# A matrix product with GELU on one core: groups 8 to 15 worked in pairs of the same block of A

## The chip, the cores and the metric

The kernel runs on 1 core of one Trainium2 chip. The metric is the device time of one execution in microseconds. Before the change it is 1500.78 us (median of 3 runs, 1499.52 to 1502.21).

## The reference

Two float32 matrices of 4096 x 4096 are multiplied and the tanh form of GELU is taken of the product.

```python
x = np.matmul(a, b)
return 0.5 * x * (1 + np.tanh(np.sqrt(2 / np.pi) * (x + 0.044715 * x**3)))
```

The kernel computes the product with float16 operands and float32 sums. It also sums the squares of the inputs, and a flag that it works out from them at the end decides whether a slower general path has to follow; in the runs here it does not.

## The kernel before

**Outer scheme.** A and B are each split into four quadrants (11, 12, 21, 22). Instead of eight products of quadrants the kernel makes seven, P1 to P7, after Strassen and Winograd: P1 and P2 are products of plain quadrants, the others take sums and differences of them. Of A these are S1 = 21 + 22, S2 = S1 - 11, S3 = 11 - 21 and S4 = 12 - S2; the products use P1: 11, P2: 12, P3: S4, P4: 22, P5: S1, P6: S2, P7: S3. The sums of B are worked out in the first groups and kept in DRAM as units (tiles `k_unit`, [128, 4, 2048] of float16, four cells of 512 KB each), so the later groups only fetch them.

**Groups.** A quadrant of A is 2048 rows high; it is worked in 4 blocks of 512 rows (mb), and a quadrant of B in 4 blocks of 512 columns (nb). A group is one pair (mb, nb): all seven products for 512 rows and 512 columns of each quadrant, 16 output tiles of 128 x 512. There are 16 groups in the order mb 0 to 3, four each; the blocks of B are taken in turned order, so that the last block of one mb is the first of the next. Group 0 is written out by hand (`first_group`), groups 1 to 6 load B and make its sums (`raw_group`), groups 7 to 15 fetch units (`late_group`).

**A product, uncut or cut.** One product is [512 x 2048] times [2048 x 512] into 4 PSUM banks, one for each row tile of 128. Uncut ("u") it is 4 quarters in K of 16 matmuls of 512 columns (`quarters`, `products`, L563): 64 matmuls. Cut, it is itself done by the seven-product scheme (`split`, `stage`, `part_pe`, L955): seven parts of 16 matmuls of 256 columns, 112 half-width matmuls in place of 64 whole ones. A cut product has 4 stages: stage 1 does part 1, stage 2 parts 2 and 5, stage 3 parts 6 and 7, stage 4 parts 3 and 4. Between them inner sums are made on VectorE (DVE), each 128 x 2048 float16 (`combine2`, L871):

- of A up to four: for part 5, then 6 and 3 (made in place of the one before), and 7 (`inner_sum`);
- of B four (`prepare` in `made_here`, mode "m", in place; `made_stored`, mode "ms", in other cells and stored to DRAM as pieces). Mode "f" fetches seven pieces instead, and "um" is an uncut product whose fetched unit is made into pieces beside it.

Where several groups of the same block of A cut the same product, the first can rewrite one quarter of the block in place (`BASE`, "make"), and the others ("made") need three inner sums of A instead of four. With a base, the sum for part 6 is not needed.

The parts are joined in PSUM: after part 1 its result (in the banks of region 21) is copied to region 11 and region 12 is set to zero (`copy_part`, L968, ScalarE, one instruction for each half bank, 128 x 256); after part 5 region 12 is copied out (j5); between parts 6 and 7 region 21 is copied out (j2); after part 7 two sums are added into the regions (`add_part`, L972, DVE, again one for each half bank). The first two matmuls of part 1 can be wide (`bits`): they run over 512 columns, which lets a following product add onto the whole bank.

**Order of the work.** PSUM has two sets of 4 banks, X and Y. Two products run interleaved (`run`, `both`): a stage or quarter of the one, then one of the other. In `late_group` these are two products of the same group: P1 with P2, P6 with P5, P7 with P3, and P4 alone or with the next group's P1 (`pending`). Their results are taken out by ScalarE (`copy_out`, L1166) or added on DVE (`add_bank`, L1172), then go through GELU (L1150) and a store on the queue of SP.

Everything from group 1 on is first listed with costs in `Plan` and then put in order by `schedule`: PE keeps the order in which products were listed; every other engine and both DMA queues (SP for stores, POOL for loads) take, at each step, the ready instruction with the earliest due time. The result is one fixed order of instructions for each engine. `MARGIN` is what the plan adds to the landing of a DMA before a DVE or ScalarE instruction counts as ready.

**Turning A.** Groups 7 and 11 load the next block of A in half blocks of 4 DMAs each through two free chunks (`turn_quad`); two DVE transposes (L440) and eight ScalarE weighings (L1206) of each half block follow.

**Cells.** SBUF holds 28 cells of 512 KB: 16 for B, 8 for S1 and S2, 4 for S3; there are 15 small tiles of 128 x 512 float32 (`y`).

Of the kernel before, what the change touches and what calls it, by code (L numbers as in the profile page):

```python
# [67 lines left out]
MARGIN = 0.6  # L68
# [21 lines left out]
def modes_of(tail=None, early=None, first4=None, **kw):  # L90
    got = {name: mode for mode, names in kw.items() for name in names.split()}
    return {**got, **{k: v for k, v in (("tail", tail), ("early", early), ("first4", first4)) if v}}


def bases_of(all_modes):
    got = {}
    for gs in (tuple(range(N_RAW, 8)), (8, 9, 10, 11), (12, 13, 14, 15)):
        early = [g for g in gs if all_modes[g].get("early") == "start"]
        turn = gs[-1] in TURNS
        for name in NAMES:  # L100
            if turn and (name in ("P2", "P6") or early and name in ("P1", "P5")):
                continue
            own = [g for g in gs if not (name == "P3" and (g in TURNS or g in early))]
            found = []
            while own and all_modes[own[-1]].get(name, "u") in ("f", "m", "ms"):
                found.append(own.pop())
            if len(found) > 1:
                for g in found:
                    got[g, name] = "made"
                got[found[-1], name] = "make"  # L110
    return got
# [16 lines left out]
TURNS = {7: 2, 11: 3}  # L128
# [191 lines left out]
def half_path(  # L320
# [39 lines left out]
    PS = [[psum_pool.tile([P, NC], F32, name="acc", tag=f"acc{k}{i}") for i in range(RT)] for k in range(2)]  # L360
# [65 lines left out]
    def turn_a(quad, c, h=None):  # L426

        x = slice(0, NX) if h is None else slice(h * NX // 2, (h + 1) * NX // 2)
        if (quad, c) == THIRD:
            n = NX // RT  # L430
            parts = [(slice(i * n, (i + 1) * n), staged[quad, c][i]) for i in range(x.start // n, x.stop // n)]
        else:
            parts = [(x, staged[quad, c][:, x, :])]
        for x, src in parts:
            transpose(a_slot[quad], c, x, src)

    def transpose(slot, c, x, src):
        dst = a_phys[slot, c].bitcast(U32).rearrange("p jj (mb q) -> p jj mb q", q=Q)
# [116 lines left out]
    def bank(s, i):  # L555
        return PS[s][i][:, :]
# [250 lines left out]

    def new_small():
# [22 lines left out]
    def fetch_unit(nb, name, q):  # L831
        x = new_cell()
        dma("POOL", cell(x), unit(nb, name)[:, q, :], [("u", nb, name, q)], [c(x)], "unit")
# [16 lines left out]


# [31 lines left out]
    def inner_sum(op, x, y, t=None):  # L883
        t = new_cell() if t is None else t
# [51 lines left out]
    def region(s, hw, r):  # L936
        h, w = int(hw[0]) - 1, int(hw[1]) - 1
        return PS[s][2 * h + r][:, w * HC : (w + 1) * HC], ("p", s, 2 * h + r)

    def part_pe(z, p):  # L940
# [8 lines left out]
        for r in range(2):  # L949
            i = 2 * h + r  # L950

            def fn(i=i, r=r):
                for j in range(NJ):
                    wide = p == "1" and j == 0 and z.bits
                    nc.tensor.matmul(  # L955
                        PS[s][i][:, :] if wide else PS[s][i][:, w * HC : (w + 1) * HC],
# [6 lines left out]
        if p in z.sum and p != "6" and z.last:  # L963
            free_cells.append(z.sum.pop(p))
# [4 lines left out]

    def add_part(dst, x, y):  # L970
        (d, dt), (xa, xt), (ya, yt) = dst, x, y
        dve("part", lambda: nc.vector.tensor_tensor(out=d, in0=xa, in1=ya, op=ALU.add), [xt, yt], [dt])  # L972

    def stage(z, k):
        s = z.s

        def of(hw, r):
            return region(s, hw, r)

# [4 lines left out]
        if k == 1:  # L984
# [7 lines left out]
            for r in range(2):  # L992
                copy_part(of("11", r), of("21", r))
            for r in range(2):
                copy_part(of("12", r), (zeros[:, 0:1].to_broadcast([P, HC]), None), "zero")
            z.prepare(1)
        elif k == 2:
            part_pe(z, "2")
            x5 = z.sum["5"]
            part_pe(z, "5")  # L1000
            if z.last:
                free_cells.remove(x5)
# [182 lines left out]
    def turn_quad(mb, quad, slot, pairs):  # L1185
# [3 lines left out]
        for h in range(2):  # L1189
# [9 lines left out]
            for cc in range(CH):  # L1199
                src = s.rearrange("p x (c r) -> p c x r", c=CH)[:, cc]  # L1200
                x = slice(h * n, (h + 1) * n)
                dve("turn", lambda cc=cc, x=x, src=src: transpose(slot, cc, x, src), toks, [("a", slot, cc, h)])
            f = new_small()
            for x in range(n):
# [3 lines left out]
                    toks, [("rows", ih), ("f", f)], batch=("w", mb, quad, h), slack=60.0)  # L1208
# [135 lines left out]
    def raw_group(gi, keep_units, makes, fetch=(), next_nb=None, turn=None, pending=None):  # L1344
# [47 lines left out]
        if turn:  # L1392
# [4 lines left out]
            turn_quad(turn, "11", slots["a"]["21"], (24, 26))  # L1397
# [23 lines left out]
        if turn:  # L1421
            turn_quad(turn, "12", slots["a"]["11"], (24, 26))
# [16 lines left out]
        if turn:  # L1439
            turn_quad(turn, "21", slots["a"]["12"], (24, 26))  # L1440
# [37 lines left out]
        def p4_ends():  # L1478
            if turn:
                turn_quad(turn, "22", slots["a"]["22"], (24, 26))  # L1480
# [46 lines left out]
    sets, held_sums = {"X": 0}, []  # L1527
    BASE = bases_of(GROUPS)

    def late_group(gi, modes, turn=None, pending=None):  # L1530

        mb, nb = groups[gi]
        new_mb = gi == N_RAW or groups[gi - 1][0] != mb
        last = gi == LAST
        X, Y = sets["X"], 1 - sets["X"]
        cut = {name for name in NAMES if modes.get(name, "u") in ("f", "m", "ms")}
        p4_first = bool(turn) or "first4" in modes
        if p4_first:
            cut.discard("P4")
        tail_v = "P7" in cut or "P3" in cut and modes.get("tail") == "v" or "P4" in cut  # L1540
        tail_v = tail_v or pending is not None and not p4_first
        if gi == N_RAW:
            for q in range(QPH):
                copy_quarter(ST[q], raw("21"), q)
        elif new_mb:
            block(SA, 1, raw("21"), raw("22"))
        if new_mb or not held_sums:
            block(SB, -1, blk(SA), raw("11"))
        s3 = ST
        if new_mb and gi != N_RAW:  # L1550
            block(ST, -1, raw("11"), raw("21"))
        def early():
            k = new_unit()
            turn_quad(groups[gi][0] + 1, "11", slots["a"]["21"], (k[0], k[2]))
            free_cells.extend(k)

        held_sums.clear()
        s4_in_slot = not turn and modes.get("early") != "start"
        if modes.get("early") == "start":
            early()  # L1560
        if s4_in_slot:
            if new_mb:
                s4 = raw("21")
                for q in range(QPH):
                    dst, toks = a_quarter(s4, q)
                    combine2(dst, toks, a_quarter(raw("12"), q), a_quarter(blk(SB), q), -1)
            held_sums.append(gi)
        if turn:
            k = new_unit()
            pairs = (k[0], k[2])  # L1570

        def fourth():
            if not s4_in_slot:
# [318 lines left out]
```

## Time and profile before

| | before |
|---|---|
| median of the runs shown | 1500.78 us |
| the profiled execution | 1500.4 us |
| its span | 1498.5 us |
| mean granted TensorE clock | 0.998 |
| PE, DVE, ACT, POOL busy | 1483.8, 1207.5, 708.8, 452.6 us |
| matmuls | 9886 |
| DMA traffic | 388.76 MB |

The span runs from the first to the last instruction; the profiled execution's own time is 1.9 us longer. PE is the row of the matmuls, PEld the weight loads that run beside them. Matmuls are pipelined, so the mean length of one (379 ns for 512 columns) is not the time between two; that is read from the chain of work or from a stretch of the timeline, by the start of the first and the number that follow. In the rows of groups, the number behind the bar is the idle time of that engine just before those instructions, with what ended it.

### The profile page before, as it was taken

The numbers are of one execution on the slowest core, as the hardware profiler recorded it, in microseconds if no ns is written. First come the engines' busy times: TensorE is split into PE (matmuls) and PEld (weight loads), VectorE is DVE, ScalarE is ACT, GpSimd is POOL, SyncE is SP. The second block draws the span as 40 slices with busy tenths as digits, with TensorE's granted clock in tenths as the row PEclk, the third lists the DMA queues.
The fourth block names the chain that finished last, engine by engine and source line by source line (L and its number), as shares of the span: only waits on it lengthen the run. The fifth ranks groups of instructions, "written<-read, shape, count | busy, mean of one in ns | idle before, by whom it ended". The sixth has DMA issues, their size and how long they took to land.

```text
span 1498.5 us, 26219 instructions
## 1 busy us (share of the span) xinstructions
PE 1483.8 (99%) x9886; PEld 967.4 (65%) x9886; DVE 1207.5 (81%) x1476; ACT 708.8 (47%) x1606; POOL 452.6 (30%) x822
## 2 busy tenths in 40 slices
PE   9999999999999999999999999999999999999997
PEld 4444554444445446555665888887765778888886
DVE  2598778246499889686799999998699889998887
ACT  5445246363954645546663242436654234242433
POOL 7766342451204415212330212122331112112220
PEclk9999999999999999999999999999999999999999
DMA  9999799999979999997997777889997747698974
GB/s 177 193 204 224 135 247 314 292 279 268 249 269 250 284 356 254 309 264 239 252 330 297 269 265 241 299 272 215 305 283 288 259 141 264 209 336 279 327 257 182
DMA packets 200918, 388.76 MB, mean 259 GB/s; under 512 B 20304, under 2 KB 110416, under 8 KB 200784
## 3 DMA queue, kind: packets, MB, share of 16 engines
q0 software_dynamic: 139296, 231.79, 65.3%
q1 hardware_dynamic: 61488, 155.22, 27.5%
q8 instruction: 79, 1.29, 0.3%
q14 instruction: 55, 0.45, 0.1%
HBM read 315.62 MB, written 155.19 MB: 314 GB/s over the span
## 4 chain that ended last, share of the span: by engine, by line
PE 90%; DMA 5%; POOL 2%; DVE 1%; ACT 1%; issue 1%; DVEq 0%; ACTq 0%; POOLq 0%
PE acc L563 47%; PE acc L955 43%; DMA stage<-in_a_dram 2%; DMA bR<-k_unit 2%; POOL bR L465 1%; POOL stage L465 1%; DVE bR L871 0%; POOL aD L465 0%; DVE y L1172 0%; DMA out_dram<-y 0%; ACT stage L474 0%; DMA aD<-in_a_dram 0%; DMA bR<-in_b_dram 0%; ACT y L1150 0%; ACT y L1206 0%
## 5 line engine op out<-in xcount | busy, mean ns | idle before, releaser
L563 PE MATMUL acc<-bR,aT 128*128 128x512 f16 x1792 | 393.6, 379 | 1.0 <-DVE y L1172 0.6
L871 DVE TENSOR_TENSOR bR<-bR 128x2048 f16<-128x2048 f16 (+1 forms) x292 | 344.7, 1203 | 47.1 <-PE acc L955 23.6
L789 POOL DMA_DIRECT2D bR<-k_unit x258 | 143.7, 559 | 629.7 <-PE acc L955 359.3
L563 PE MATMUL acc<-bR,aD 128*128 128x512 f16 x1472 | 322.4, 379 | 0.0
L563 PEld LDWEIGHTS <-aT 128*128 128x128 f16 x1856 | 181.6, 98 | 215.0 <-issue 1.6
L955 PE MATMUL acc<-bR 128*128 128x256 f16 x2640 | 307.3, 273 | 1.5 <-ACT y L968 1.5
L955 PEld LDWEIGHTS <-bR 128*128 128x128 f16 x2640 | 258.3, 98 | 33.6 <-issue 1.6
L563 PEld LDWEIGHTS <-aD 128*128 128x128 f16 x1568 | 153.3, 98 | 182.5 <-DVE aD L548 1.2
L1172 DVE TENSOR_TENSOR y<-acc,y 128x512 f32<-128x512 f32 x324 | 209.0, 684 | 36.0 <-ACT y L1166 14.7
L789 POOL DMA_DIRECT2D bR<-in_b_dram x288 | 155.5, 545 | 252.5 <-DMA bR<-in_b_dram 102.2
L955 PE MATMUL acc<-bR,aT 128*128 128x256 f16 (+1 forms) x1696 | 201.0, 274 | 0.0
L968 ACT COPY y<-acc 128x256 f32<-128x256 f32 x220 | 81.6, 372 | 238.2 <-PE acc L955 235.4
L955 PEld LDWEIGHTS <-aT 128*128 128x128 f16 x1696 | 166.0, 98 | 24.4
L1150 ACT ACTIVATE y<-y 128x512 f32<-128x512 f32 x200 | 119.9, 626 | 109.0 <-DVE y L1172 108.7
L1240 ACT ACTIVATE y<-bR 128x1024 bf16<-128x1024 f16 x128 | 129.8, 1052 | 66.0 <-DVE y L1245 51.9
L1245 DVE TENSOR_TENSOR y<-y 128x1024 bf16<-128x1024 bf16 x120 | 82.1, 686 | 41.6 <-ACT y L1240 40.1
L955 PE MATMUL acc<-bR,aD 128*128 128x256 f16 (+1 forms) x944 | 110.9, 273 | 0.0
L955 PE MATMUL acc<-bR,stage 128*128 128x256 f16 (+1 forms) x880 | 105.7, 274 | 0.0
L955 PEld LDWEIGHTS <-aD 128*128 128x128 f16 x944 | 92.4, 98 | 12.1
L955 PEld LDWEIGHTS <-stage 128*128 128x128 f16 x880 | 86.1, 98 | 15.1
L871 DVE TENSOR_TENSOR bR<-aT 128x2048 f16<-128x2048 f16 x66 | 80.3, 1217 | 18.2 <-PE acc L563 18.2
L1166 ACT COPY y<-acc 128x512 f32<-128x512 f32 x80 | 45.9, 586 | 103.2 <-PE acc L563 65.4
(89 smaller groups left out, 1223.4 us busy)
## 6 DMA issues: line engine op xcount, KB each, us to landing
bR<-k_unit POOLq DMA_DIRECT2D x258, 512.0 KB, 7.0
out_dram<-y SPq DMA_DIRECT2D x252, 256.0 KB, 7.0
k_unit<-bR SPq DMA_DIRECT2D x112, 512.0 KB, 8.8
bR<-in_b_dram POOLq DMA_DIRECT2D x384, 128.0 KB, 6.9
k_piece<-bR SPq DMA_DIRECT2D x40, 512.0 KB, 4.7
bR<-in_a_dram POOLq DMA_DIRECT2D x64, 256.0 KB, 8.9
stage<-in_a_dram POOLq DMA_DIRECT2D x48, 256.0 KB, 7.7
bR<-k_piece POOLq DMA_DIRECT2D x24, 512.0 KB, 7.7
```

Of the source, the lines that this page charges most:

```text
L465: nc.gpsimd.dma_start(out=dst, in_=src)
L563: nc.tensor.matmul(acc, sa[:, j // 2, i * P : (i + 1) * P, j % 2], sb[:, j, :], start=start and j == 0, stop=stop and j == 3, skip_group_c ...
L789: return plan.add(queue, COST[queue], lambda: eng.dma_start(out=dst, in_=src), r=r, w=w, size=MOVE[what] * SPREAD, weight=weight, **kw)
L871: nc.vector.tensor_tensor(out=dst, in0=xa, in1=ya, op=ALU.add if op > 0 else ALU.subtract)
L955: nc.tensor.matmul(PS[s][i][:, :] if wide else PS[s][i][:, w * HC : (w + 1) * HC], sa[:, j // 2, r * P : (r + 1) * P, j % 2], rhs(j, wide) ...
L968: act(cost, lambda: nc.scalar.copy(out=d, in_=x), [xt] if xt else [], [dt])
L1150: act("gelu", lambda: nc.scalar.activation(t, t, ACT.Gelu_apprx_tanh), [("f", f)], [("f", f)])
L1166: act("copy", lambda: nc.scalar.copy(out=sm(f), in_=bank(s, i)), [], [("f", f), ("p", s, i)])
L1172: dve("add", lambda: nc.vector.tensor_tensor(out=sm(g), in0=bank(s, i), in1=sm(f), op=ALU.add), [("f", f)], [("f", g), ("p", s, i)])
L1240: act("square", lambda t=t, src=src: nc.scalar.activation(t, src, ACT.Square), [c(cx)], [("f", f)], slack=60.0)
L1245: dve("add16", lambda t=t, u=u: nc.vector.tensor_tensor(out=u, in0=u, in1=t, op=ALU.add), [("f", f)], [("f", e)], slack=60.0)
```

## The change

Groups 8 to 15 are worked in pairs of groups that have the same block of A: 8 and 9, 10 and 11, 12 and 13, 14 and 15. `late_pair` runs each product for both groups, one on each set of banks, interleaved: P1, P2, P6, P5, P3, P7, P4. Group 7 keeps the old way (`lone_group`).

- Where both groups cut a product, the second uses the inner sums of A that the first had made (`lead`); the sum that is made in place waits until both are through the part before. In stage 2 the second group does part 5 before part 2.
- Where both leave a product uncut, the two run one behind the other.
- An uncut product adds onto what is in its banks; where the product before was cut, the running sum is first copied back into the bank (`seed`).
- The PSUM sets become one tile of four banks each, and four of the joins are done for two banks in one instruction: the copy to region 11, the zero, the copy j5, and each of the two adds. The copy j2 stays in halves.
- The running sum u of both groups (8 small tiles) is stored to DRAM after P5 (`park`) and loaded back after P3 (`unpark`). Two cells of B become four more small tiles.
- The block of A is turned during groups 7 and 10/11; in the pair through one chunk only. S1, S2, S3 and S4 of a new block are made by 16 sums at its start (`fill`); in the turning pair S4 is made over S2 after P6.
- `MARGIN` goes from 0.6 to 0.2.
- The tables say anew which products are cut and how, in the raw groups too, and which pieces groups 4 and 5 make; `bases_of` looks at whole pairs of pairs.

```diff
-MARGIN = 0.6
+MARGIN = 0.2
 def bases_of(all_modes):
...
+    for a, b in ((8, 10), (12, 14)):
         for name in NAMES:
+            if b == 10 and name in ("P2", "P3", "P6"):
                 continue
...
+            if all(all_modes[g].get(name, "u") in ("f", "m", "ms") for g in (a, a + 1, b, b + 1)):
+                got[a, name], got[b, name] = "make", "made"
-RAW_MAKES = {4: ("P1", "P4", "P3"), 5: ("P2",)}
-RAW_CUT = {4: "P7", 5: "P7 P3", 6: "P7", 2: "", 1: "P7"}
+RAW_MAKES = {4: ("P6", "P5", "P2"), 5: ("P4",)}
+RAW_CUT = {4: "P3", 5: "P7", 6: "P7", 2: "", 1: "P3"}
 GROUPS = {
-    7: modes_of(m="P1 P6", ms="P7", tail="v"),
-    8: modes_of(f="P7", m="P3 P4 P6", ms="P5", um="P2"),
-    9: modes_of(f="P3", m="P1 P4 P5 P6 P7", ms="P2"),
-    10: modes_of(m="P1 P2 P3 P5 P7", ms="P6", early="end"),
-    11: modes_of(m="P1 P2 P6 P7", tail="v"),
-    12: modes_of(m="P4 P6 P7", ms="P5", tail="v"),
-    13: modes_of(f="P7", m="P1 P2 P3 P4 P5 P6"),
-    14: modes_of(f="P3", m="P2 P6 P7", ms="P1 P4 P5"),
-    15: modes_of(f="P2 P6", m="P1 P4 P5 P7", ms="P3", tail="v", first4=True),
+    7: modes_of(m="P1 P6", um="P4", tail="v"),
+    8: modes_of(m="P2 P3 P4 P5 P6 P7", ms="P1"),
+    9: modes_of(f="P5", m="P2", ms="P6 P7", um="P3"),
+    10: modes_of(f="P4", m="P1 P2 P5 P6 P7"),
+    11: modes_of(m="P1 P4 P5 P7"),
+    12: modes_of(m="P1 P2 P3 P4 P6", ms="P5 P7"),
+    13: modes_of(f="P1", m="P2 P3 P4 P5 P7", ms="P6"),
+    14: modes_of(f="P2 P3 P6", m="P4 P5 P7", ms="P1"),
+    15: modes_of(m="P1 P2 P3 P5 P6", ms="P7"),
 }
-TURNS = {7: 2, 11: 3}
+EXTRA = (14, 15)
+PARK = (8, 10, 12, 14)
+TURNS = {7: 2, 10: 3}
...
-    PS = [[psum_pool.tile([P, NC], F32, name="acc", tag=f"acc{k}{i}") for i in range(RT)] for k in range(2)]
+    PS = [psum_pool.tile([P, RT, NC], F32, name="acc", tag=f"acc{k}") for k in range(2)]
...
             part_pe(z, "1")
-            for r in range(2):
-                copy_part(of("11", r), of("21", r))
-            for r in range(2):
-                copy_part(of("12", r), (zeros[:, 0:1].to_broadcast([P, HC]), None), "zero")
+            copy_pair(pair_of("11"), pair_of("21"))
+            copy_pair(pair_of("12"), (zeros[:, 0:1].unsqueeze(2).to_broadcast([P, 2, HC]), []))
...
-            part_pe(z, "2")
             x5 = z.sum["5"]
-            part_pe(z, "5")
+            for p in "25" if z.first else "52":
+                part_pe(z, p)
...
-            for r in range(2):
-                copy_part(j(z.j5, r), of("12", r))
+            copy_pair(pair_j(z.j5), pair_of("12"))
...
-            for r in range(2):
-                add_part(of("12", r), of("12", r), j(j2, r))
+            add_pair(pair_of("12"), pair_of("12"), pair_j(j2))
...
-            for r in range(2):
-                add_part(of("22", r), of("21", r), j(z.j5, r))
+            add_pair(pair_of("22"), pair_of("21"), pair_j(z.j5))
...
+    def late_pair(ga, turn):
+        gs = (ga, ga + 1)
...
+        if groups[ga - 1][0] != mb:
+            fill("S1", 1, "21", "22")
+            fill("S2", -1, "S1", "11")
+            fill("S3", -1, "11", "21")
+            if not turn:
+                fill("21", -1, "12", "S2")
...
+        def both(name, fresh, dones, bits):
+            lists, cuts, lead = [], [], None
+            for s in range(2):
...
+                shared = is_cut(0, name) and is_cut(1, name)
+                z = split(s, source[name], b, bits(s), BASE.get((ga, name)) if shared else None, lead)
+                lead = z if shared else None
+                lists.append(stages_of(z, lambda i, s=s: dones(s, i)))
...
+        new_a("11", "21")
+        both("P1", lambda s: True, p1_done, uncut("P2"))
+        new_a("21", "11")
+        if last:
+            final_answer()
+        both("P2", cut("P2"), p2_done, uncut("P6"))
+        both("P6", cut("P6"), p6_done, uncut("P5"))
+        if last:
+            final_read()
+        if turn:
+            fill("S2", -1, "12", "S2")
+        new_a("22", "12")
+        both("P5", cut("P5"), p5_done, uncut("P3"))
+        if ga in PARK:
+            park()
+        new_a("12", "S1")
+        both("P3", cut("P3"), p3_done, lambda s: False)
+        if ga in PARK:
+            unpark()
+        both("P7", lambda s: True, p7_done, uncut("P4"))
+        both("P4", cut("P4"), p4_done, lambda s: False)
```

More of the change, by code (lines that the diff above doesn't have):

```diff
@@ L1525, in raw_group @@
         return later_
-    sets, held_sums = {"X": 0}, []
     BASE = bases_of(GROUPS)
[L1530 to L1535, printed above, removed]
-        cut = {name for name in NAMES if modes.get(name, "u") in ("f", "m", "ms")}
[L1537 to L1573, printed above, removed]
-                block(SB, -1, raw("12"), blk(SB))
@@ L1726, in late_group, with c22, c21 @@
[L1726 removed]
+            f = new_small()
+            add_bank(v[i], X, i, f)
+            out_of(gi, i, 1, 1, f)
+        def c22(i):
+            f = copy_out(X, i)
+            add_bank(f, Y, i)
+            out_of(gi, i, 1, 1, f)
+        def c21(i):
+            add_bank(x4[i], X, i)
+            out_of(gi, i, 1, 0, x4[i])
+        run(work("P4", Y, True, p4_done))
+        turn_quad(turn, "22", raw("22"), pairs)
+        turn_quad(turn, "11", blk(ST), pairs)
```

379 lines of the change are left out of this document (199 added, 180 removed).

## The prediction

> **What bounds the kernel now.** The first view to read is the page's table of busy times, because its shares say which engine can set the end at all, and then the waits of PE, which say whether that engine ever stood still.
>
> ```profile
> PE 1483.8 (99%) x9886; PEld 967.4 (65%) x9886; DVE 1207.5 (81%) x1476; ACT 708.8 (47%) x1606; POOL 452.6 (30%) x822
> DVE  2598778246499889686799999998699889998887
> DMA  9999799999979999997997777889997747698974
> ...
> PE acc L955 <- ACT y L968: 1.5, 1, 1.5
> PE acc L572 <- DVE table L744: 1.5, 1, 1.5
> PE acc L598 <- ACT y L581: 0.7, 1, 0.7
> PE acc L563 <- DVE aD L548: 0.7, 1, 0.7
> PE acc L563 <- DVE y L1172: 0.6, 1, 0.6
> PE acc L598 <- DMA bR<-in_b_dram: 0.4, 1, 0.4
> PE acc L563 <- DMA bR<-k_unit: 0.4, 1, 0.4
> PE acc L563 <- ACT y L581: 0.4, 1, 0.4
> ```
>
> PE waits 6.2 us in the whole span. L572 and L598, and the waits on aD at L548 and y at L581, belong to the first group, which the change leaves alone; what is left after it is 1.5 + 0.6 + 0.4 = 2.5 us. A busy PE could still be a slow one, so the next view is the chain that ended last, where runs of matmuls show their pace without a gap, and the groups by form, which count the matmuls.
>
> ```profile
> 178.27 1.96 PE acc L955 x16
> 707.43 1.75 PE acc L955 x16
> 1130.77 3.45 PE acc L563 x16
> 1134.23 3.49 PE acc L955 x32
> ...
> L955 PE MATMUL acc<-bR,aT 128*128 128x512 f16 x24 | 9.1, 379 | 0.0
> L955 PE MATMUL acc<-bR,stage 128*128 128x512 f16 x14 | 5.3, 379 | 0.0
> L955 PE MATMUL acc<-bR,aD 128*128 128x512 f16 x2 | 0.8, 379 | 0.0
> L968 ACT COPY acc<-zero 128x256 f32<-128x256 f32 x110 | 41.1, 375 | 3.1
> ```
>
> One quarter of an uncut product (16 matmuls of 512) takes 3.45 us, so an uncut product takes 4 x 3.45 = 13.80 us. Two parts of a cut product (32 matmuls of 256) take 3.49 us, so its seven parts take 3.5 x 3.49 = 12.22 us, and a cut is worth 1.58 us of PE. Where the first matmuls of part 1 are wide, the part takes 1.96 instead of 1.75 us: 0.21 us more. Two zero copies stand in each cut product, so 110 of them are 55 cuts, and two wide matmuls stand in each wide one, so 24 + 14 + 2 = 40 are 20 wide cuts. This checks against GROUPS and RAW_CUT: 5 cuts in the raw groups, 50 in groups 7 to 15.
>
> Since PE is paced by its own matmuls nearly everywhere, a change can win only three things: matmul time, the 2.5 us of late waits, and what follows the last matmul. The tail is in the timeline of the last stretch.
>
> ```profile
> 1484.30 7.33 DVE L1172 TENSOR_TENSOR y<-acc,y 128x512 f32<-128x512 f32 x12
> 1485.01 7.28 ACT L1150 ACTIVATE y<-y 128x512 f32<-128x512 f32 x12 [3.35 <-DVE y L1172]
> 1488.08 1.91 PE L955 MATMUL acc<-bR,aT 128*128 128x256 f16 x16
> ```
>
> The last matmul ends at 1488.08 + 1.91 = 1489.99, the last add at 1491.63, the last gelu at 1492.29, and the span at 1498.5 with the last store.
>
> **The change, part by part.**
>
> Matmuls. Counting the names in the new tables: raw groups 4 cuts (was 5), group 7 two (was 3), groups 8 to 15 7 + 4 + 6 + 4 + 7 + 7 + 7 + 6 = 48 (was 47). That is 54 against 55, +1.6 us. A cut product starts wide where the next product in its banks adds onto it: the 4 raw ones, P6 of group 7, and in the pairs P1 of 11, P5 of 9, 10 and 11, P7 of 9 and 15, so 11 against 20: 9 x 0.21 = -1.9 us. Together -0.3 us on the path. The order of the products is free on PE.
>
> Tail. Now 12 adds in 7.33 us, 0.61 each, are queued on DVE around the last parts, and the last one ends 1.64 us behind the last matmul. In the new order the last thing is the fourth quarter of group 15's uncut P4, whose four row tiles end 0.86 us apart (3.45/4), each with one add; only one add is left behind the last matmul, 0.68 us by the row of L1172 below. I take -0.9 us; the bounds are 0 and -1.6.
>
> DVE. The groups by form give busy time, mean ns of one, and idle time before; the last two rows are one of the windows (busy PE, PEld, DVE, ACT, POOL, then clock, DMA share, GB/s) and one of the chain.
>
> ```profile
> L871 DVE TENSOR_TENSOR bR<-bR 128x2048 f16<-128x2048 f16 x284 | 339.8, 1218 | 47.1 <-PE acc L955 23.6 <-PE acc L563 9.2 <-DMA bR<-in_b_dram 6.4
> L1172 DVE TENSOR_TENSOR y<-acc,y 128x512 f32<-128x512 f32 x324 | 209.0, 684 | 36.0 <-ACT y L1166 14.7 <-PE acc L955 10.8 <-PE acc L563 5.6
> L972 DVE TENSOR_TENSOR acc<-acc,y 128x256 f32<-128x256 f32 x220 | 83.8, 424 | 10.2 <-ACT y L968 5.2 <-PE acc L955 4.4
> L968 ACT COPY y<-acc 128x256 f32<-128x256 f32 x220 | 81.6, 372 | 238.2 <-PE acc L955 235.4
> L1166 ACT COPY y<-acc 128x512 f32<-128x512 f32 x80 | 45.9, 586 | 103.2 <-PE acc L563 65.4 <-issue 20.1 <-PE acc L955 17.1
> ...
> 800.00:1000.00 200.00, 200.00 (x1767) 172.59 (x1765) 194.70 (x243) 73.39 (x175) 37.19 (x67) 1.00 0.75 264
> 1473.70 4.62 DVE bR L871 x4
> ```
>
> Of A, a cut product makes four inner sums (three where a base is "made"). Before: 50 late cuts, 25 of them "made", and one more shares (P4 of 14 and 15): about 200 - 25 - 3 = 172 sums. After: 21 products are shared by both groups of a pair, 8 of these "made", and 8 cuts stand alone: 13 x 4 + 8 x 3 + 8 x 4 = 108. So 64 sums go, at 4.62/4 = 1.16 us each 74 us of DVE. The sums of B stay (44 cuts make theirs, 6 fetch them, as before). The joins: four adds of 424 ns become two of the 128x512 form, 684 ns, 1.70 to 1.37 us per cut; on ACT six copies of about 372 become three of about 586 with j2 still in halves. All of this is worth nothing on the path: in the row 800:1000 DVE is busy 194.7 of 200 us while PE is busy 200.00, so PE does not wait even for a full DVE. If that cover went, it would be where DVE is fullest in the new kernel, the pair 12 and 13: 52 sums of B, 28 of A, 16 for the blocks of A, 28 joins and 56 adds, 96 x 1.16 + 84 x 0.61 = 162 us against 14 x 12.22 = 171 us of PE, 95%, under the 97% that the row shows covered.
>
> A pair operation reads or writes two banks, so it cannot start until both row tiles of the part are done. Timed from the start of two interleaved cuts: part 1 of the first ends at 1.75, the two-bank copy and the zero follow (two of 586 ns, at 2.9), and part 2 wants the banks at 3.5, after part 1 of the second. 0.6 us is left; I count 0, and above 0 only where ACT is late (below). The page "PSUM — Partial Sum Buffer" of the Trainium skill (PSUM bank collisions raise a hardware error) has it that engines are to be kept apart by whole bank and not by address, so that PE stays out of both banks until the copy and the zero are done, though part 2 writes only a half of each. By that rule the 0.6 us is all there is; by address the zero would not matter and 1.2 us would be left, and the sum is the same by both. No row here shows PE and ACT in one bank at once.
>
> Shared sums. This adds a wait that the old kernel did not have. Without a base (P2 and P6 of 8/9, P1 and P4 of 10/11, P4 of 12/13) the sum for part 6 is made in place of the sum for part 5, once the second group is through part 5. By the times above: second group's stage 2 begins at 7.0, its part 5 (now first) ends at 8.75, the sum of 1.22 us ends at about 10.0, and the first group's part 6 starts at 10.5. Before, the same sum had from 7.0 on. The sum for part 3 behind part 6 has the same half microsecond. Behind it on DVE wait the sums of B for part 7. It costs 0 if DVE is free at that moment, and if it is in the middle of another sum up to 1.16 - 0.5 = 0.66 us, at 10 places: 0 to 6.6 us, and no gain. I take 0, by the nearest row (a DVE at 97% with no PE wait).
>
> Moves. Parking u adds 4 x 8 stores on SP and as many loads on POOL, of 256 KB. The page's DMA lines and a window beside them:
>
> ```profile
> DMA packets 200918, 388.76 MB, mean 259 GB/s; under 512 B 20304, under 2 KB 110416, under 8 KB 200784
> ...
> out_dram<-y SPq DMA_DIRECT2D x252, 256.0 KB, 7.0
> ...
> 700.00:800.00 100.00, 100.00 (x630) 61.49 (x629) 81.86 (x94) 63.59 (x165) 31.19 (x57) 1.00 1.01 292
> ```
>
> That is 16.8 MB more over some 690 us, 24 GB/s. A parked tile is back after two landings of 7.0 us, and P3's two products (24 us) lie between; the queue of POOL issues 8 more in a stretch where it is 30% busy. In 700:800 the DMA engines are busy without a break and PE still does not wait. Cost 0, bounds 0 and one wait of 0.4 us per pair (as the wait on k_unit above), 1.6 us. The page "DMA: Bandwidth & Descriptors" (Specifications) speaks against this part: it gives HBM about 358 GB/s per core. By it the 24 GB/s on top of a slice at 292 still fits and the sum stays; the fastest slice, 356 GB/s in the page of before, would not have room.
>
> Waits behind a DMA. MARGIN goes from 0.6 to 0.2 us, so DVE and ACT instructions that read fresh data are queued closer to its landing, and A is turned through one chunk instead of two. What that costs when it fails is in the waits: the 1.5 us at L968.
>
> ```profile
> 1125.57 0.63 ACT L1206 ACTIVATE y<-bR 128x512 f16<-128x512 f16 x1 [2.97 <-DMA bR<-k_unit]
> 1128.46 0.63 ACT L968 COPY y<-acc 128x256 f32<-128x256 f32 x2
> 1128.87 1.91 PE L955 MATMUL acc<-bR 128*128 128x256 f16 x16 [1.48 <-ACT y L968]
> ```
>
> A weighing of A stood 2.97 us on ACT, the copy out of the bank queued behind it came late, and PE stood 1.48 us. The new kernel has the same 16 half blocks of A to turn behind group 6. I take the three late waits (2.5 us) as replaced by as much, net 0; the bounds are -2.5 and +9 (six such waits more).
>
> **Sum.** -0.3 - 0.9 + 0 = -1.2 us. The profiled execution took 1500.4 us (span 1498.5), so 1499.2 there; its median of runs is 1500.78, 0.4 above, so 1499.6.
>
> **Rivals.** A: all late waits go, the freed DVE being early everywhere. Then -1.2 - 2.5 = -3.7, 1497.1 us. For it: 74 us less on DVE. Against: two of the three waits (1.5 and 0.4) hang on a DMA, and DVE's relief does not move a landing. Lower than this it cannot go by much, as the matmuls stay.
>
> B, on the other side: the shared sums without a base are late. One place is nothing; from 7 of the 10 places (4.6 us) on, it outweighs the 1.2 us and 3 us more. At all ten 1499.6 + 6.6 = 1506.2 us. For it: 0.5 us of room, where a sum takes 1.16. Against: the row 800:1000, where DVE is 97% full and no sum came late for PE.
>
> C, also slower: landings are late by more than the new margin and ACT's weighings hold the copies, 1.5 us each as in the row above. From three more on it is slower; six give 1499.6 + 9 = 1508.6 us. For it: 0.4 us less margin, one chunk, 16.8 MB more. Against: before, with a full queue, it happened once.
>
> **Numbers.** My forecast, no change in effect, 0.45. A 0.2. B 0.14, C 0.16; 0.05 for something in neither. A measurement of this kernel tells about 0.2%, 3 us. Faster 0.21, same 0.45, slower 0.34. The likeliest case alone goes from 1497.8 to 1503.8. The range reaches over A and to the end of C: 1496.6 to 1508.6.
>
> **What would show it.** The matmuls: 110 zero copies of 128x256 become 54 of 128x512, and the wide matmuls at the line of the parts are 22. The tail: one add after the last matmul. DVE near 1207 - 83 = 1125 us busy. PE's waits: few, none above 1.5 us; B shows as waits of PE's part 6 or 3 on a DVE sum in pairs 8, 10 and 12, C as waits on an ACT copy behind a weighing in group 7 or pair 10, or on k_unit. The forecast is wrong if PE's late waits sum to more than 7 us or to less than 1.

## The result and the profile after

The kernel after takes 1846.13 us (median of 4 runs, 1845.62 to 1848.18), the kernel before beside it 1500.15 us (4 runs, 1498.86 to 1502.21). The ratio is 1.2307, with an interval from 1.2286 to 1.2329: 23% slower. The profiled execution took 1845.62 us with a span of 1844.1 us, so 345.6 us more span than before.

The page of the kernel after, with the busy times, and the busy tenths of PE over 40 slices of the span:

```profile
PE 1550.4 (84%) x9838; PEld 963.5 (52%) x9838; DVE 1115.3 (60%) x1260; ACT 691.3 (37%) x1452; POOL 470.7 (26%) x854
...
PE   8778888888888898888888888888988878787876
```

PE, 99% busy before, is 84% busy, and DVE and ACT have lower shares than before too: no engine has become the bound. The loss is spread over the whole span: already the second slice shows 7, and it belongs to the first group. So the pairs cannot be the cause alone. A stretch of 640 us that lies ahead of the first pair in the kernel after, and ahead of group 8 in the kernel before, in the windows of both kernels (columns: busy us and count of PE, PEld, DVE, ACT, POOL, then clock, DMA share, GB/s); of the kernel after:

```profile
60.00:700.00 640.00, 550.31 (x2602) 254.33 (x2601) 374.68 (x414) 267.01 (x525) 199.52 (x366) 1.00 0.88 210
```

and of the kernel before:

```profile
60.00:700.00 640.00, 638.28 (x3229) 315.67 (x3227) 480.70 (x560) 331.11 (x629) 230.57 (x423) 1.00 1.05 261
```

The clock is 1.00 in both, and 2602 matmuls are done instead of 3229. What PE stood for is in its waits (us in total, times, longest), kernel after:

```profile
PE acc L964 <- DVE y L1187: 58.3, 61, 1.4
PE acc L964 <- ACT y L978: 34.0, 73, 0.7
PE acc L964 <- DVE acc L997: 32.4, 28, 1.2
PE acc L559 <- ACT y L1181: 29.9, 43, 1.2
PE acc L559 <- ACT y L1175: 23.6, 33, 1.2
PE acc L559 <- DVE y L1187: 21.8, 25, 1.4
...
PE acc L594 <- DVE y L573: 10.6, 13, 0.8
```

All lines of this view together are 375 waits and 287.0 us, against 8 waits and 6.2 us before. Nearly all of the releasers are instructions that read or write PSUM: the adds onto results, the copies out, the joins. Hardly any of them was late before, and L594 with L573 is the first group, whose code the change leaves as it was, but for the PSUM line and the way its banks are addressed.

What such a wait looks like is in the timeline of the first group (start, duration, engine, line, instruction, and in brackets the idle time before it and its releaser). Kernel after:

```profile
18.74 0.59 ACT L577 COPY y<-acc 128x512 f32<-128x512 f32 x1
...
19.38 1.02 PE L594 MATMUL acc<-bR,aT 128*128 128x512 f16 x4 [0.67 <-ACT y L577]
...
20.43 0.59 ACT L577 COPY y<-acc 128x512 f32<-128x512 f32 x1 [1.11 <-PE acc L594]
21.07 1.02 PE L594 MATMUL acc<-bR,aT 128*128 128x512 f16 x4 [0.68 <-ACT y L577]
```

and the same place before:

```profile
15.63 10.74 PE L598 MATMUL acc<-bR,aT 128*128 128x512 f16 x49
...
18.54 1.76 ACT L581 COPY y<-acc 128x512 f32<-128x512 f32 x3
```

Before, PE runs 49 matmuls without a break while ACT copies three finished banks out beside it. After, PE does the four matmuls of a row tile, ACT copies that row tile out, and only then does PE start on the next one, which lies in another bank. The two take turns: a row tile comes every 1.69 us (21.07 - 19.38). Late in the kernel DVE and PE do the same:

```profile
1509.17 1.03 PE L964 MATMUL acc<-bR,aD 128*128 128x256 f16 x8 [0.78 <-DVE y L1187]
...
1510.24 0.69 DVE L1187 TENSOR_TENSOR bR<-acc,y 128x512 f32<-128x512 f32 x1 [1.12 <-PE acc L964]
...
1510.99 1.03 PE L964 MATMUL acc<-bR,aD 128*128 128x256 f16 x8 [0.78 <-DVE bR L1187]
```

Here 8 matmuls take a turn of 1.82 us (1510.99 - 1509.17) where 8 of them in an unbroken run take 3.49/4 = 0.87 us.

**Where the 345.6 us are.** PE is idle for 1844.1 - 1550.4 = 293.7 us against 14.7 before: 279.0 us. The other 66.6 us (1550.4 - 1483.8) stand as busy time, although 48 matmuls fewer were done. Most of them come from the end of each run in front of a wait. The four matmuls above start 0.215 us apart from the first on, as in an unbroken run (16 in 3.45), so the start costs nothing; but behind the last one no other starts, and its whole length shows, 0.379 us: 3 x 0.215 + 0.379 = 1.02 us, where a share of an unbroken run is 0.86. The reader starts only when that last one is through (20.43, after 19.38 + 1.02 = 20.40). That is 0.16 us for each of 375 waits, 60 us as an estimate.

### The profile page after: what moved, and what is told of

Its sections match the earlier page's. It is cut to its first block, busy times and chain, and to the rows that moved or that the text cites. A ratio compares the mean times of both kernels' runs of the same rounds, so it can differ in the third digit from the quotient of the medians.

```text
span 1844.1 us, 25848 instructions
## 1 busy us (share of the span) xinstructions
PE 1550.4 (84%) x9838; PEld 963.5 (52%) x9838; DVE 1115.3 (60%) x1260; ACT 691.3 (37%) x1452; POOL 470.7 (26%) x854
## 5 line engine op out<-in xcount | busy, mean ns | idle before, releaser
L559 PE MATMUL acc<-bR,aT 128*128 128x512 f16 x1792 | 406.6, 379 | 62.8 <-ACT y L1181 16.4
L879 DVE TENSOR_TENSOR bR<-bR 128x2048 f16<-128x2048 f16 (+1 forms) x296 | 344.6, 1192 | 89.2 <-PE acc L559 45.8
L964 PE MATMUL acc<-bR 128*128 128x256 f16 x2688 | 321.7, 272 | 67.9 <-DVE acc L997 32.4
L559 PEld LDWEIGHTS <-aD 128*128 128x128 f16 x1568 | 153.9, 98 | 240.4 <-issue 66.4
L1187 DVE TENSOR_TENSOR y<-acc,y 128x512 f32<-128x512 f32 x237 | 155.9, 687 | 152.0 <-PE acc L964 79.6
L964 PE MATMUL acc<-bR,aD 128*128 128x256 f16 (+1 forms) x1056 | 128.5, 275 | 29.6 <-DVE y L1187 24.0
L1165 ACT ACTIVATE y<-y 128x512 f32<-128x512 f32 x158 | 96.3, 630 | 140.2 <-DVE y L1187 140.0
L997 DVE TENSOR_TENSOR acc<-acc,y 128x512 f32<-128x512 f32 x92 | 64.3, 699 | 109.6 <-PE acc L964 60.1
L964 PEld LDWEIGHTS <-aD 128*128 128x128 f16 x1056 | 103.7, 98 | 51.1 <-issue 34.7
L978 ACT COPY y<-acc 128x256 f32<-128x256 f32 x96 | 35.7, 373 | 181.1 <-PE acc L964 181.1
L964 PE MATMUL acc<-bR,stage 128*128 128x256 f16 x656 | 78.9, 273 | 12.1 <-ACT y L978 3.7
L1222 ACT ACTIVATE y<-bR 128x512 f16<-128x512 f16 x120 | 75.7, 631 | 5.5 <-DMA bR<-in_a_dram 2.7
```

Of the source, the lines that this page charges most:

```text
L559: nc.tensor.matmul(acc, sa[:, j // 2, i * P : (i + 1) * P, j % 2], sb[:, j, :], start=start and j == 0, stop=stop and j == 3, skip_group_c ...
L879: nc.vector.tensor_tensor(out=dst, in0=xa, in1=ya, op=ALU.add if op > 0 else ALU.subtract)
L964: nc.tensor.matmul(PS[s][:, i, :] if wide else PS[s][:, i, w * HC : (w + 1) * HC], sa[:, j // 2, r * P : (r + 1) * P, j % 2], rhs(j, wide) ...
L978: act(cost, lambda: nc.scalar.copy(out=d, in_=x), [xt] if xt else [], [dt])
L997: dve("add", lambda: nc.vector.tensor_tensor(out=d[0], in0=x[0], in1=y[0], op=ALU.add), [*x[1], *y[1]], d[1])
L1165: act("gelu", lambda: nc.scalar.activation(t, t, ACT.Gelu_apprx_tanh), [("f", f)], [("f", f)])
```

## The experiments

The one line of the diff that reaches all groups is that of PSUM: eight tiles of one bank became two tiles of four banks. **Theory T**: the waits written into the program follow the tile, not the bank, so PE waits for whatever ACT or DVE has to read in any other bank of its set. The views infer a releaser from semaphore events, and for the first matmul of a row tile they name ACT or DVE. The rivals: **H**, the order of the pairs costs it; **J**, the two-bank joins hold PE up; **M**, a PSUM tile of several banks is slow by itself; **B** and **C** of the prediction, late shared sums and late landings. All kernels were compared with the kernel before on the same chip.

**One tile per bank again (e1), all else of the change kept.** Joins over two banks can't be written then, so these are in halves again.

```diff
-    PS = [psum_pool.tile([P, RT, NC], F32, name="acc", tag=f"acc{k}") for k in range(2)]
+    PS = [[psum_pool.tile([P, NC], F32, name="acc", tag=f"acc{k}{i}") for i in range(RT)] for k in range(2)]
...
-            copy_pair(pair_of("11"), pair_of("21"))
+            for r in range(2):
+                copy_part(of("11", r), of("21", r))
```

(and likewise the zero, j5, the two adds, and the places that address the banks)

> The changed kernel with its PSUM as eight tiles of one bank again and the joins in halves; pairs, shared sums, parking, tables and margin stay. Theory T (a tile of PSUM is the unit for which waits are set, so that PE waits in each bank for what is read from the bank before): the 340 us go, 1497 to 1504 us, PE waits under 10 us. Rival H (the order in pairs itself, by late shared sums, parking or landings): it stays above 1800 us.

Measured: 1501.45 us (10 runs, 1499.47 to 1505.43) against 1501.16, ratio 1.0004 [0.9988, 1.0020]. The pairs, the shared sums, the parking, the new tables and the margin are all in it, so none of them costs the 346 us; H, B and C fall as causes. Its busy times and waits (page, then waits of PE):

```profile
PE 1485.0 (99%) x9838; PEld 962.3 (64%) x9838; DVE 1114.2 (74%) x1368; ACT 706.7 (47%) x1614; POOL 469.7 (31%) x854
```

```profile
PE acc L559 <- DVE y L1182: 1.9, 2, 1.8
PE acc L964 <- DVE bR L879: 1.7, 3, 0.8
PE acc L568 <- DVE table L740: 1.5, 1, 1.5
PE acc L964 <- DVE aD L879: 1.1, 1, 1.1
PE acc L964 <- DVE aT L879: 1.1, 1, 1.1
PE acc L964 <- DVE acc L982: 0.8, 1, 0.8
PE acc L594 <- DMA bR<-in_b_dram: 0.6, 1, 0.6
```

The 375 waits are 11.

**Only the PSUM line in the kernel before (e2).**

```diff
-    PS = [[psum_pool.tile([P, NC], F32, name="acc", tag=f"acc{k}{i}") for i in range(RT)] for k in range(2)]
+    PS = [psum_pool.tile([P, RT, NC], F32, name="acc", tag=f"acc{k}") for k in range(2)]
...
-        return PS[s][i][:, :]
+        return PS[s][:, i, :]
```

(and likewise in the other places that address the banks)

> The kernel before with nothing changed but its PSUM: two tiles of four banks in place of eight of one, joins in halves as before. T: as slow as the changed kernel, 1780 to 1880 us, with PE waits of 0.6 to 1.4 us behind reads of ACT and DVE from group 0 on. H: no change, 1500 us.

Measured: 1840.25 us (4 runs) against 1501.16, ratio 1.2262 [1.2222, 1.2301]. The line alone, with no pair and no two-bank join, makes the whole loss, +339 us, with the same kind of waits. The traces of e2 and of the kernel before list the same instructions of PE, DVE and ACT in the same order (9886, 1476 and 1606); only the waits between them differ. So no other order of the work is hidden in the line:

```profile
PE acc L955 <- DVE y L1172: 64.4, 72, 1.8
PE acc L955 <- DVE acc L972: 35.2, 40, 1.0
PE acc L955 <- ACT y L968: 34.5, 75, 0.5
```

**Tiles of four banks, joins in halves (e4).** The kernel after with the edit of the joins from e1 and without that of PS.

```diff
-            copy_pair(pair_j(z.j5), pair_of("12"))
+            for r in range(2):
+                copy_part(j(z.j5, r), of("12", r))
...
-            add_pair(pair_of("12"), pair_of("12"), pair_j(j2))
+            for r in range(2):
+                add_part(of("12", r), of("12", r), j(j2, r))
```

> The changed kernel with its two tiles of four banks, but the joins in halves, as before. T: the width of the joins is not it, 1830 to 1900 us, a little above the changed kernel because there are more reads to wait for. A rival J (a join over two banks is what holds PE): 1500 to 1560 us.

Measured: 1861.81 us, ratio 1.2400 [1.2359, 1.2441], above the interval of the kernel after. Against J: the joins over two banks are not what holds PE up, since without them the kernel is no faster but 15.7 us slower (1861.81 - 1846.13). One row of waits is larger with the half adds:

```profile
PE acc L964 <- DVE acc L982: 49.4, 50, 2.1
```

It stood at 32.4 us with the joins in one (L997 above). Other rows shrank, and all waits of PE together are 293.3 us against 287.0, only 6.3 more. The rest of the difference lies in PE's busy time (1563.6 against 1550.4 us), in executions with a lower granted clock (0.989 against 0.995, down to 0.97 between 800 and 1000 us). How much of the 15.7 us the joins themselves save is therefore open.

**Four tiles of two banks (e3)**, joins over two banks kept.

```diff
-    PS = [psum_pool.tile([P, RT, NC], F32, name="acc", tag=f"acc{k}") for k in range(2)]
+    PS = [[psum_pool.tile([P, 2, NC], F32, name="acc", tag=f"acc{k}{h}") for h in range(2)] for k in range(2)]
```

(and likewise in the places that address the banks)

> The changed kernel with four tiles of two banks, the joins still for two banks at once. T: the serial chain is cut in two, since a bank waits only for its neighbour: between, 1620 to 1720 us. H: above 1800 us.

Measured: 1597.14 us, ratio 1.0644 [1.0609, 1.0679]. The direction is T's, the size is not: the loss is 96 us and not the 120 to 220 that I had expected. What is left of it has one main row, the copy j2 in halves between the parts 6 and 7:

```profile
PE acc L964 <- ACT y L978: 44.1, 95, 0.7
```

**Which banks share a tile (e5 and e6).** Both are the kernel before with two-bank tiles; in e5 the row tiles 0 and 2, and 1 and 3 share one, in e6 the neighbours 0 and 1, and 2 and 3, which are one region.

```diff
-    PS = [[psum_pool.tile([P, NC], F32, name="acc", tag=f"acc{k}{i}") for i in range(RT)] for k in range(2)]
+    PS2 = [[psum_pool.tile([P, 2, NC], F32, name="acc", tag=f"acc{k}{h}") for h in range(2)] for k in range(2)]
+    PS = [[PS2[k][i % 2][:, i // 2, :] for i in range(RT)] for k in range(2)]
```

(e5; in e6 the last line has `PS2[k][i // 2][:, i % 2, :]`)

> The kernel before with two banks to a tile of PSUM, the banks of row tiles 0 and 2 in one tile and of 1 and 3 in the other, so that neighbours in time lie in different tiles. T (PE waits for whatever is read from another bank of the same tile): almost nothing is read from bank 0 while PE writes bank 2, 1500 to 1512 us. Rival M (any tile of more than one bank costs by itself): 1560 us or more, as in the next run.

> The same with row tiles 0 and 1 in one tile and 2 and 3 in the other. T: PE waits in every second bank, 1570 to 1650 us (the changed kernel with such tiles took 1597). M: the same as the run before it.

Measured: e5 1556.51 us, ratio 1.0376 [1.0350, 1.0402]; e6 1599.58 us, ratio 1.0675 [1.0646, 1.0704]. The waits of e6 and a place in its timeline:

```profile
PE acc L956 <- ACT y L969: 50.6, 110, 0.5
```

```profile
1000.75 0.37 ACT L969 COPY y<-acc 128x256 f32<-128x256 f32 x1 [1.10 <-PE acc L956]
1001.18 1.03 PE L956 MATMUL acc<-bR 128*128 128x256 f16 x8 [0.46 <-ACT y L969]
1002.25 0.37 ACT L969 COPY y<-acc 128x256 f32<-128x256 f32 x1 [1.12 <-PE acc L956]
...
1002.67 2.78 PE L956 MATMUL acc<-bR 128*128 128x256 f16 x24 [0.46 <-ACT y L969]
```

110 waits are two for each of the 55 cuts. After part 6, PE waits for the copy j2 of the first row tile, does its part 7 (8 matmuls), waits for the copy of the second, and goes on. The second copy itself waits for those 8 matmuls, though they write the bank beside the one it reads. At 0.16 us more for the end of each run (above) these 110 waits are 68 of the 98 us that PE's idle and busy time grew by (1596.5 - 1498.5). With a tile per bank the copy of the one row tile lies beside the matmuls of the other. In e5 these two banks are in different tiles, and PE waits for none of these copies, at the same size of tile. So the two kernels differ by 43 us at the same size of tile, and M falls: the price is not that of a larger tile but of which readers share it with which matmuls. What is left in e5 is waits too: 61 of them, 48.6 us in all, are 42.4 us more than before, and with 0.16 us for each of the 53 further waits that is an estimate of 51 of the 56.9 us of span. My expectation for e5, 1500 to 1512, missed all the same, because I had thought only of the joins. Its main wait is another pairing:

```profile
PE acc L956 <- DVE y L1173: 24.5, 28, 1.4
```

These are adds onto results that are still queued on DVE when PE wants the other bank of the tile.

**No shared sums (e7).** From e1, with each group making its own inner sums. This kernel leaves out that a base is rewritten only once: where a quarter of the block is rewritten in place, both groups rewrite it.

```diff
-                lead = z if shared else None
+                lead = None
```

> The changed kernel with one-bank tiles, and each group of a pair makes its own inner sums of A: 64 sums more on DVE, 74 us, and one to two more cells held in each product. If the relief of DVE is worth nothing because it lay beside PE (the prediction's reading): 1500 to 1506 us. If the order in pairs needs it (DVE at 95% in 12 and 13 without these sums spared, no cell to spare): 1520 to 1560 us.

Measured: 1546.29 us, ratio 1.0319 [1.0290, 1.0349]: 47.5 us above the kernel before on the same chip, where e1 was 0.3 above it. Page, then waits of PE:

```profile
PE 1495.0 (97%) x9838; PEld 963.9 (62%) x9838; DVE 1195.5 (77%) x1444; ACT 708.7 (46%) x1614; POOL 469.9 (30%) x854
```

```profile
PE acc L964 <- DMA bR<-k_unit: 16.6, 10, 4.0
PE acc L964 <- DVE acc L982: 8.3, 5, 5.6
```

DVE has less to do here than before the change (1195.5 against 1207.5 us), and yet joins come 5.6 us late and cells of B are loaded late. So the new order needs the shared sums: without them the pairs do cost time. Whether they help by the time of DVE that they spare or by the cells was not separated: each product also holds one or two cells more here, and the largest row of waits is for loads into cells.

**The old margin (e8).** From e1, for rival C.

```diff
-MARGIN = 0.2
+MARGIN = 0.6
```

> The changed kernel with one-bank tiles and MARGIN at 0.6 again. By rival C of the prediction (instructions of DVE and ACT queued too close to a landing hold PE): 1495 to 1500 us, below the 1501 with 0.2. If landings are not what PE waits for there (its waits name sums and adds of DVE): no gain, 1501 to 1509 us, since a later due time only pushes work back.

Measured: 1505.45 us, ratio 1.0041 [1.0029, 1.0054], where e1 was 1.0004 [0.9988, 1.0020]. The wider margin does not help; the smaller one is not what C took it for.

**The late waits of e1 eased (e11), and a cut more (e12).** In e11, P7 of group 10 and P4 of group 14 make their sums of B in other cells, and the weighings of A get a later due time (`SLACK`). In e12, from e11, the margin is 0.4, group 5 cuts P3 in place of P7, and of the last pair group 14 makes P1 and P4 in place and group 15 cuts P4 too: 55 cuts instead of 54.

```diff
-    10: modes_of(f="P4", m="P1 P2 P5 P6 P7"),
+    10: modes_of(f="P4", m="P1 P2 P5 P6", ms="P7"),
-    14: modes_of(f="P2 P3 P6", m="P4 P5 P7", ms="P1"),
+    14: modes_of(f="P2 P3 P6", m="P5 P7", ms="P1 P4"),
-SLACK = 60.0
+SLACK = 120.0
```

> The changed kernel with one-bank tiles, and P7 of group 10 and P4 of group 14 with their sums of B in other cells (ms for m), and the weighings given more time (SLACK 120). If the 4 us of PE waits on sums and adds of DVE are all that keeps the order in pairs from its floor (prediction's rivals B against A): 1495.5 to 1498.5 us, against about 1500 for the kernel before, PE's late waits under 3 us. If they only move elsewhere: 1500 to 1503 us.

```diff
-MARGIN = 0.2
+MARGIN = 0.4
-RAW_CUT = {4: "P3", 5: "P7", 6: "P7", 2: "", 1: "P3"}
+RAW_CUT = {4: 'P3', 5: 'P3', 6: 'P7', 2: '', 1: 'P3', 3: ''}
-    14: modes_of(f="P2 P3 P6", m="P5 P7", ms="P1 P4"),
-    15: modes_of(m="P1 P2 P3 P5 P6", ms="P7"),
+    14: modes_of(f="P2 P3 P6", m="P1 P4 P5 P7"),
+    15: modes_of(m="P1 P2 P3 P5 P6", ms="P4 P7"),
```

> The same with P4 of group 15 cut (55 cuts, as before the change), MARGIN 0.4 and P3 instead of P7 cut in group 5. One more cut is 1.58 us less of PE and the wide start of P7 goes, 0.21 us: 1494 to 1498 us if the waits stay as in the run before it; 1499 to 1502 us if the last product of all is now a cut one whose adds stand behind the last matmul (1.6 us of tail as in the kernel before) and the sums of P4 come late.

Measured: e11 1501.53 us, ratio 1.0015 [1.0005, 1.0025]; e12 1504.00 us, ratio 1.0033 [1.0017, 1.0049]; the kernel before took 1498.9 us beside them. e11 is in the second of its two ranges, waits that only move; e12 is above both of its ranges. PE's waits, of e11:

```profile
PE acc L559 <- DVE y L1182: 2.5, 2, 2.3
...
PE acc L964 <- DVE aD L879: 1.1, 1, 1.1
PE acc L964 <- DVE stage L879: 1.1, 1, 1.1
```

and the first of e12:

```profile
PE acc L559 <- DVE y L1182: 3.5, 1, 3.5
```

The waits behind the sums were 3.9 us in e1 (1.7 + 1.1 + 1.1) and are 2.2 in e11, while those behind the adds grew from 1.9 to 2.5: waits moved more than they went, and the time against the kernel before did not fall. A cut is worth 1.58 us of PE, but the median of e12 is 2.5 us above that of e11, with one add 3.5 us late. The two intervals overlap, so this difference is hardly clear of noise, and which of the edits would cost it wasn't separated. No version with pairs was faster than the kernel before.

## Why the prediction was wrong

1499.6 us was forecast, 1496.6 to 1508.6 as the range, and 1846.13 came. **The step that failed is the one on the two-bank joins**: it counted what a join over two banks needs ("0.6 us is left; I count 0"), and it gave the PSUM line no term of its own, though that line also changes every matmul and every read outside the joins. "The first group, which the change leaves alone" was wrong for the same reason. What the runs showed in its place: e2 and e1 put the line on the one kernel and take it off the other, and 339 and 345 us come and go with it.

Most of the rows for a bound stood in the prediction. The rows there that read or write the banks on DVE and ACT are 209.0 + 83.8 + 81.6 + 45.9 + 41.1 = 461.4 us; three more of the kernel before, the copies to region 11 (39.1), GELU straight from a bank (23.3) and the copies from bank to bank of the raw groups (18.1), bring the groups after the first to 541.9 us, nearly all of it covered by matmuls in other banks. If that cover goes, the cost lies between 0 and an estimate of some 540 us, and the measured 345.6 is inside. Asking of the PSUM line "name the work that hides it" would have found the bound; it did not need any unseen price. The sentence "No row here shows PE and ACT in one bank at once" looked for the wrong row: the one that mattered shows them in different banks at once, 15.63 in the timeline of before.

The rule weighed there, of the Trainium skill, "PSUM — Partial Sum Buffer" (PSUM bank collisions raise a hardware error), asks only that engines be kept apart by bank. The row of before agrees that PE and ACT in different banks go on side by side: 49 matmuls in 10.74 us. The kernel after is held far wider than this rule asks.

Point by point, by e1, which has everything but that line and the two-bank joins:

- **Matmuls.** The forms were as counted: 54 zero copies and 12 + 8 + 2 = 22 wide matmuls. Rows of the groups by form, kernel after:

```profile
L994 ACT COPY acc<-zero 128x512 f32<-128x512 f32 x54 | 31.8, 589 | 1.5
...
L964 PE MATMUL acc<-bR,aD 128*128 128x512 f16 x12 | 4.5, 379 | 0.8 <-DVE y L1187 0.8
L964 PE MATMUL acc<-bR,aT 128*128 128x512 f16 x8 | 3.0, 379 | 0.0
L964 PE MATMUL acc<-bR,stage 128*128 128x512 f16 x2 | 0.8, 379 | 0.0
```

- **Tail.** Right in its form, larger in size. The timeline of the end of e1:

```profile
1490.50 3.62 PE L559 MATMUL acc<-bR,aT 128*128 128x512 f16 x16
...
1494.16 0.69 DVE L1182 TENSOR_TENSOR bR<-acc,bR 128x512 f32<-128x512 f32 x1 [0.17 <-PE acc L559]
1494.88 0.63 ACT L1160 ACTIVATE bR<-bR 128x512 f32<-128x512 f32 x1 [0.23 <-DVE bR L1182]
```

  One add is left, and it ends 0.73 us behind the last matmul (1494.85 - 1494.12), where 1.64 stood: the forecast 0.9. Beyond that, the stretch from the last gelu to the end is 4.9 us instead of 6.2, which the forecast left out. From the last matmul to the end it is 6.3 instead of 8.5 us: -2.2.
- **DVE.** About 1125 us was forecast; 1115.3 came in the kernel after and 1114.2 in e1. The sums at the line of `combine2` went from 608 to 544, the 64 that were counted. That the relief is worth nothing on the path was right against the old order, and e7 shows that the new order would cost 47 us without the sharing. The forecast had asked only what the relief adds, not what the new order needs.
- **The full pair.** DVE was to be at 95% in the pair 12 and 13. The fullest stretch of 200 us in e1, which covers most of that pair, has 182 us, 91% (the window 1100 to 1300 of e1):

```profile
1100.00:1300.00 200.00, 196.83 (x1798) 175.38 (x1797) 181.97 (x240) 78.19 (x188) 45.57 (x82) 1.00 0.81 290
```

  PE is covered there but for 3.2 us, where the row of before that I went by (800 to 1000, with a fuller DVE) had none.
- **Shared sums without a base.** I took 0 with a bound of 6.6, and the term itself was right. In e1 PE waits 3.9 us for sums at L879, but mostly for others. The two longest waits are for sums that write into the block of A itself. One of them, in the timeline of e1:

```profile
1222.41 1.23 DVE L879 TENSOR_TENSOR aD<-bR,aD 128x2048 f16<-128x2048 f16 x1 [0.20 <-PE acc L964]
...
1223.69 1.49 PE L964 MATMUL acc<-bR,aD 128*128 128x256 f16 x12 [1.10 <-DVE aD L879]
```

  The sum reads a quarter of the block (`aD`) and an inner sum (`bR`) and writes `aD`: by the kernel's lines it is the one that rewrites a quarter in place for a base, in P5 of the pair 12 and 13. DVE stands 0.20 us until PE lets it start, and PE, whose next matmuls read `aD` too, then stands 1.10 us until the sum is done. The other such place is at 1273.01, in P7 of that pair, also 1.10 us. These 2.2 us are a wait that the prediction did not price: it had only the sums without a base as rivals. Of the other three waits, two (0.80 and 0.73 us) are for sums made in cells of B, and only the last, 0.17 us at 1131.27, is for a sum made in place of another without a base. So rival B's mechanism cost next to nothing in e1.
- **Parking.** No row of PE's waits in e1 names it: 0, as taken. The room that the prediction doubted was there: the fastest slice of e1 moves 362 GB/s, beyond the 356 of before.
- **Margin and landings.** Net 0 holds: late waits are 6.8 us in e1 (8.9 in all, less the 1.5 and 0.6 of the first rows of work) against 2.5, but only 0.6 us of all waits is for a landing, and e8 is not faster. The longest late wait is 1.8 us, where none above 1.5 was forecast.
- **Sum.** In e1 the last matmul ends 4.1 us later than before (1494.12 against 1489.99): waits of PE +2.7 (8.9 - 6.2) and its busy time +1.2, where -0.3 was forecast. The tail takes 2.2 back, so the span is 1.9 us longer, 1500.4 against 1498.5. So the forecast of no change holds for the change without its PSUM line and its two-bank joins (ratio 1.0004), but in part by luck: terms of both signs were each larger than I took them, and they nearly cancel. The two traces are single executions, and the runs of e1 spread over 6 us.

What stays open: whether the joins over two banks would gain anything if PE's waits stayed by bank. It wasn't tried: a join over two banks needs one tile over both, and with the tile the waits come.

## What to carry to other kernels

In this kernel a PSUM tile is also the unit of waiting: give each bank that one engine fills while another empties its neighbour a tile of its own, and price any line that merges tiles by all the reads that lie beside matmuls in the kernel before, not by the instructions it was written for. An edit to an allocation reaches code that the diff does not show; look for a stretch that the change does not touch otherwise (here the first group) and ask whether it could move. Where relief of a covered engine is "worth nothing", ask also whether the new order could do without it.

## What the runs showed of the hardware that was not expected

- Each run of matmuls that ends in front of a wait shows about 0.16 us more as busy, the length of its last matmul beyond the step from one start to the next (0.379 against 0.215 us): four matmuls of 512 columns took 1.02 us where 0.86 is their share of an unbroken run. By the estimate above this is most of the 66.6 us by which PE's busy time grew; idle time alone would have given 279.0 of the 345.6.
- Handing a bank to a reader and back costs PE little more than the read itself: it stands 0.78 us for an add of 0.69, and 0.46 for a copy of 0.37. With the full length of the last matmul, 1.03 us for 8 matmuls of 256 columns, PE and DVE in turns need 1.82 us for 0.87 us of matmuls.
- The granted clock fell little with PE's gaps: 0.995 over the span, where it was 0.998. It was lowest in e4, 0.989.
